# Five single-use weight buffers kept in the ring, 8 KB rows for the last expert's second weights, and another order in the first stages of a one-core block kernel

## The chip, the cores and the metric

The kernel runs on one core of a Trainium2 chip. The metric is the device time of one execution in microseconds. Before the change three runs took 1821.74, 1823.43 and 1823.79 us, so the median is 1823.43 us.

## The reference, cut to what matters

Two transformer blocks on 256 tokens of width 1024, in fp32. The first mixes by a gated 31-tap convolution and neighbourhood attention and ends in a mixture of 16 experts, each on its 32 best tokens. The second (sparse attention, a multi-layer perceptron, latent attention, a second perceptron) is not touched by the change.

```python
sh1, sc1, g1, sh2, sc2, g2 = adaln(c, w_mod[l], b_mod[l])
h = modulate(rms_norm(x, norm_mix_g[l]), sh1, sc1)
hc = modulate(rms_norm(ctx, norm_mix_g[l]), csh1, csc1)
u, q, k, v = jnp.split(h @ w_in[l], splits, axis=-1)
k_c, v_c = jnp.split(hc @ w_in[l][:, splits[1]:], 2, axis=-1)
y_conv = conv_mixer(u, conv_w[l], conv_b[l], conv_ln_g[l], conv_ln_b[l])
y_attn = na_attention(q, k, v, k_c, v_c, rpb[l], idx)
x = x + g1 * (jnp.concatenate([y_conv, y_attn], axis=-1) @ w_out[l])
x = x + g2 * ec_moe(modulate(rms_norm(x, norm_ffn_g[l]), sh2, sc2), ...)
```

An expert is `silu(xs @ w_gate) * (xs @ w_up)` and then `@ w_down`. Its three matrices hold 8 MB each, and every byte of them is read once.

## The kernel before, in words

**Order.** The order of the work on each engine is that in which the program text records it (a manual schedule). Each engine works its instructions off in that order; an instruction that waits holds up everything behind it on its engine.

**Weights.** All weights go through one list `loads` (L105 to L182), nearly all pieces of 1 MB, in the order of use. `pump` (L203) issues the next load on SP's queue as soon as its buffer is free, `take` (L219) hands a landed piece to the code, `free` (L226) gives its buffer back. SP's queue is in order: a load whose buffer is still read holds back all behind it. L187 to L199 give every load a kind of buffer. Ten buffers form the ring (`rp1` with 6, `rp2` with 4). While expert 0 and 1 are loaded there are eleven more on the right side of the memory, which the first stages used till then: five pools of one buffer for the loads `RS` = 9, 13, 14, 10, 12 (counted from expert 0's first load, number 0) and `rp2b` with six for the loads 15 to 20. Each of these eleven serves one load and is closed when expert 1 begins (`rs.close()`, L1010). An expert has 24 loads: `w_gate` and `w_up` in turn, 8 each (numbers 0 to 15), and 8 of `w_down` (16 to 23). So expert 1 begins at number 24.

**Last expert.** The `w_down` of expert 15 is read by column quarters, in eight loads whose rows are pieces of 1 KB (256 floats), with the four loads of `a_kvi` (the next layer's first weights) between them. A piece of a later weight is split into a high and a low part before use: ScalarE rounds it (`wh`), GpSimd or VectorE takes the rest (`wl`).

**First stages.** `w_mod` by the conditioning (`mod_part`, `mod_copy` on ScalarE, transposes on TensorE and a VectorE addition in `mod_fin`) gives the shifts and scales. `h_chunk` (L564) makes the eight chunks of the normed input, with one PSUM bank for two chunks. `half_mm` (L622) multiplies half a weight slot; `Halves` (L345) splits these halves ahead of use, with three buffers. Four rounds `s` make the gated input of the convolution, then two rounds `b` make q, then v and k follow. `drip` (L616) puts convolution taps on VectorE between other work. The sum of squares of the context runs on GpSimd (`SumSq`, L275); TensorE adds it up (`cols`) between the halves of round 2, and spreads the result (`bcast`) behind that round.

**Attention.** `pipeline` (L323) runs 8 units in a software pipeline; per step `S` (scores), `fin`, `norm` (ScalarE and VectorE scale the probabilities), `soft`, `PV`, `T` (TensorE transposes the probabilities), and then hooks (L801): the rest of `w_mod` (`mods`, `mods_b`), the layer norm of the convolution (`ln_b` to `ln_f`) and the quarters of `w_out` (`wo1`). `ln_f` (L774) is a table load, four SiLUs and a copy on ScalarE and a subtraction on VectorE. The first quarter, `wo1(0)`, doesn't read what `ln_f` writes; the second does.

## Time and profile before

| | before |
|---|---|
| median of 3 runs | 1823.43 us (1821.74 to 1823.79) |
| profiled execution, its own time | 1821.56 us |
| its span | 1819.7 us |
| TensorE busy | 1482.8 us, 81% |
| DMA, mean over the span | 300 GB/s |
| chain that ended last | DMA 49%, TensorE 40%, VectorE 6% |
| mean granted clock of TensorE | 0.878 |

The span is the time from the first to the last instruction of the profiled execution; 1.86 us of its own time lie around it. The page has busy shares in 40 slices of 45.5 us. The slices 7 to 25 (about 290 to 1145 us) are the experts, in which the DMA engines never rest; before and behind them TensorE and what it waits for set the pace.

### The profile page before, as it was taken

To read this page: it belongs to the slowest core of one execution; us is meant where nothing else is said; L and a number is where in the kernel's file an instruction comes from. 1 tells how busy PE (TensorE), PEld (TensorE's weight loads), DVE (VectorE), ACT (ScalarE), POOL (GpSimd) and SP (SyncE) were. 2 spreads that over 40 slices of the span, in tenths; PEclk is the share of its full clock that TensorE was granted. 3 is DMA by queue.
4 is the path that set the end of the run, shared out by engine and by line. 5 is a ranking of instruction groups with operands and counts; after the bars stand their busy time and mean duration, and the time that the engine had idled before them with its cause. 6 is when DMAs were issued, how large, how long until landed. Compare 5 with 4: busy or idle time off the path is not lost.

```text
span 1819.7 us, 22674 instructions
## 1 busy us (share of the span) xinstructions
PE 1482.8 (81%) x9569; PEld 905.2 (50%) x9569; DVE 547.1 (30%) x1028; ACT 425.3 (23%) x645; POOL 302.3 (17%) x137
## 2 busy tenths in 40 slices
PE   5898887677667776777677667797999998999998
PEld 2875832122111111121122111485999997889998
DVE  3894320000000000000000000378544366755333
ACT  3435410000000000000000000354454444455442
POOL 1621210000000000000000000243243334223521
PEclk8999888788788968886778788798999997999999
DMA  9639589999999999999999999971445444225550
GB/s 397 241 123 382 206 359 373 419 416 415 415 418 416 416 415 418 417 415 415 419 416 415 415 418 417 370 279 44 161 167 202 162 139 156 71 94 197 179 181 24
DMA packets 109733, 545.88 MB, mean 300 GB/s; under 512 B 8576, under 2 KB 20224, under 8 KB 68480
## 3 DMA queue, kind: packets, MB, share of 16 engines
q1 hardware_dynamic: 106656, 537.72, 74.7%
q10 hardware_dynamic: 2976, 6.72, 1.0%
q8 instruction: 75, 1.23, 0.3%
q14 instruction: 26, 0.21, 0.0%
HBM read 543.36 MB, written 1.05 MB: 299 GB/s over the span
## 4 chain that ended last, share of the span: by engine, by line
DMA 49%; PE 40%; DVE 6%; ACT 2%; issue 2%; POOL 0%; SPq 0%; ACTq 0%; DVEq 0%; POOLq 0%
DMA moe__w<-in_w_up_dram 29%; DMA moe__w<-in_w_down_dram 16%; PE mlp__psB L95 10%; PE mlp__psA L95 10%; DMA moe__w<-in_w_gate_dram 2%; PE moe__psB L95 2%; PE mlaproj__psA L95 2%; PE index__psA L95 2%; PE qkv__psA L95 2%; PE wout__psA L95 1%; PE mlawo__psA L95 1%; PE qkv__psB L95 1%; PE router__psB L95 1%; PE dsawo__psA L95 1%; PE mlaproj__psB L95 1%
## 5 line engine op out<-in xcount | busy, mean ns | idle before, releaser
L95 PE MATMUL moe__psB<-moe__w,moe__xsT 128*32 128x512 f32 x1920 | 346.2, 819 | 172.8 <-DMA moe__w<-in_w_up_dram 88.4
L95 PEld LDWEIGHTS moe__psB<-moe__w,moe__xsT 128*32 128x32 f32 x1920 | 46.7, 123 | 454.5 <-DMA moe__w<-in_w_up_dram 225.4
L95 PE MATMUL moe__psB<-moe__w,moe__hT 128*32 128x512 f32 (+1 forms) x984 | 220.3, 667 | 57.7 <-DMA moe__w<-in_w_down_dram 46.0
L1021 DVE TENSOR_TENSOR moe__hid<-moe__hid,moe__psB 128x512 f32<-128x512 f32 x15 | 10.3, 688 | 575.1 <-PE moe__psB L95 575.1
L303 POOL TENSOR_TENSOR dsaproj__wl<-moe__w,dsaproj__wh 128x1680 fp32r<-128x1680 f32 x4 | 15.2, 3795 | 939.6 <-ACT dsaproj__wh L301 939.6
L95 PEld LDWEIGHTS moe__psB<-moe__w,moe__hT 128*32 128x32 f32 x984 | 52.7, 120 | 214.9 <-DMA moe__w<-in_w_down_dram 121.7
L95 PE MATMUL mlp__psA<-mlp__hh,mlp__wl 128*128 128x256 f32 x512 | 145.0, 283 | 0.0
L95 PE MATMUL mlp__psA<-mlp__hh,mlp__wh 128*128 128x256 f32 x512 | 144.9, 283 | 0.0
L95 PE MATMUL mlp__psA<-mlp__hl,mlp__wh 128*128 128x256 f32 x512 | 144.9, 283 | 0.0
L1020 ACT ACTIVATE moe__hid<-moe__psB 128x512 f32<-128x512 f32 x15 | 9.0, 597 | 535.8 <-PE moe__psB L95 535.8
L95 PE MATMUL mlp__psB<-mlp__xgh,mlp__wh 128*128 128x256 f32 x448 | 125.5, 280 | 0.0
L95 PE MATMUL mlp__psB<-mlp__xgl,mlp__wh 128*128 128x256 f32 x448 | 125.1, 279 | 0.0
L95 PE MATMUL mlp__psB<-mlp__xgh,mlp__wl 128*128 128x256 f32 x448 | 125.0, 279 | 0.0
L301 ACT ACTIVATE mlp__wh<-mlp__w 128x2048 fp32r<-128x2048 f32 (+1 forms) x50 | 94.9, 1899 | 73.2 <-PE mlp__psA L95 55.2
L303 POOL TENSOR_TENSOR mlp__wl<-mlp__w,mlp__wh 128x2048 fp32r<-128x2048 f32 (+1 forms) x17 | 78.0, 4591 | 173.7 <-ACT mlp__wh L301 173.7
L305 DVE TENSOR_TENSOR mlp__wl<-mlp__w,mlp__wh 128x2048 fp32r<-128x2048 f32 (+1 forms) x33 | 75.7, 2292 | 87.6 <-ACT mlp__wh L301 87.6
L95 PEld LDWEIGHTS mlp__psA<-mlp__hh,mlp__wh 128*128 128x128 f32 x512 | 98.2, 192 | 0.0
L95 PEld LDWEIGHTS mlp__psA<-mlp__hh,mlp__wl 128*128 128x128 f32 x512 | 98.1, 192 | 0.0
L95 PEld LDWEIGHTS mlp__psA<-mlp__hl,mlp__wh 128*128 128x128 f32 x512 | 98.1, 192 | 0.0
L1060 DVE COPY moe__ys<-moe__psB 128x512 f32<-128x512 f32 x15 | 10.4, 691 | 251.1 <-PE moe__psB L95 251.1
L95 PEld LDWEIGHTS mlp__psB<-mlp__xgh,mlp__wh 128*128 128x128 f32 x448 | 84.2, 188 | 0.0
L95 PEld LDWEIGHTS mlp__psB<-mlp__xgh,mlp__wl 128*128 128x128 f32 x448 | 84.1, 188 | 0.0
(632 smaller groups left out, 2634.1 us busy)
## 6 DMA issues: line engine op xcount, KB each, us to landing
moe__w<-in_w_down_dram SPq DMA_DIRECT2D x123, 1024.0 KB, 20.0
moe__w<-in_w_gate_dram SPq DMA_DIRECT2D x120, 1024.0 KB, 19.9
moe__w<-in_w_up_dram SPq DMA_DIRECT2D x120, 1024.0 KB, 19.9
mlp__w<-in_mlp_down_dram SPq DMA_DIRECT2D x28, 1024.0 KB, 5.0
mlp__w<-in_mlp_up_dram SPq DMA_DIRECT2D x20, 1024.0 KB, 4.9
qkv__w<-in_w_mod_dram SPq DMA_DIRECT2D x9, 1024.0 KB, 5.1
start__w<-in_w_mod_dram SPq DMA_DIRECT2D x8, 1024.0 KB, 13.6
mod__w<-in_w_mod_dram SPq DMA_DIRECT2D x6, 1024.0 KB, 10.9
```

Of the source, the lines that this page charges most:

```text
L95: nc.tensor.matmul(o, lhsT, rhs, start=start, stop=stop, skip_group_check=True)
L301: nc.scalar.activation(h[:, 0:n], f, AF.Copy)
L303: nc.gpsimd.tensor_tensor(out=l[:, 0:n], in0=f, in1=h[:, 0:n].bitcast(F32), op=ALU.subtract)
L305: nc.vector.tensor_tensor(out=l[:, 0:n], in0=f, in1=h[:, 0:n].bitcast(F32), op=ALU.subtract)
L1020: nc.scalar.activation(hid, gp, AF.Silu)
L1021: nc.vector.tensor_mul(hid, hid, up)
L1060: nc.vector.tensor_copy(ys[1], yp[1])
```

## The change

- **Ring.** The five single-use buffers join the ring after their first load, so the loads 36 and up take turns in 15 buffers instead of 10, until the last expert's `w_down` (`n1`), whose loads use the first ten alone. `rp2b` stays a single-use pool and has a stack of its own, closed when expert 1 begins; the five are closed at the last expert.
- **Last expert.** Its `w_down` comes from a second, repacked input `w_dl`, in which each of the eight pieces has 8 KB contiguous rows. The size is the same.
- **First stages.** The first weight half is rounded ahead of `mod_copy`; the splits 2 to 4 are spread over the chunks; each chunk has a PSUM bank of its own; `cols` and the rest of the context's statistics move behind round 3, `bcast` between the halves of the first `b` round, the context's chunks from 4+4 to 3+5; `drip` does 10, 10, 12 instead of 9, 9, 11; two small VectorE products go to expert 1.
- **Attention.** `mods_b` becomes `mods_cp` (copy) and, some work later, `mods_fin` (transposes). `ln_f` moves from step 5 to step 6, behind `wo1(0)`.

```diff
-ld(1, rows(I["w_down"][e], s % 2 * 1024, slice(q * 256, (q + 1) * 256), 8), 8, 256)
+ld(1, I["w_dl"][s].rearrange("p (k f) -> p k f", k=8), 8, 256)
...
+    slots = [0] * R1 + [1] * R2
     for n, (big, _, _) in enumerate(loads):
-        if n - n0 in RS:
-            ring.append(3 + RS.index(n - n0))
-        elif n0 + RB <= n < n0 + RB + R4:
+        o = n - n0
+        if RB <= o < RB + R4:
             ring.append(2)
-        elif big:
-            ring.append(0 if nb % (R1 + R2) < R1 else 1)
-            nb += 1
+            continue
+        if o in RS:
+            ring.append(3 + RS.index(o))
         else:
-            ring.append(0)
+            if n >= n1:
+                slots = [r for r in slots if r < 2]
+            ring.append(slots.pop(slots.index(0) if not big else 0))
+        slots.append(ring[n])
...
             mod_part(mps, range(6, 8))
+            wst.ahead(1)
             mcol = mod_fin(0, mod_copy(mps))
...
-                if c % 2 == 0:
-                    hts.append(bank("B"))
-                t = half(hts[-1], c % 2)
+                t = half(bank("B"), 0)
...
-                elif s == 2:
-                    cps = bank("B")
-                    ssc.cols(cps)
-                    rc_ = stat_rs(cps)
...
-                elif s == 2:
-                    bcast(rb, rc_, T)
+                elif s == 3:
+                    cps = bank("B")
+                    ssc.cols(cps)
+                    rc_ = stat_rs(cps)
...
-                h_ctx(range(4 * b, 4 * b + 4))
+                if b:
+                    h_ctx(range(3, 8))
                 half_mm(ps, 0)
+                if b == 0:
+                    bcast(rb, rc_, T)
+                    h_ctx(range(0, 3))
                 half_mm(ps, 1)
...
-0: [mods_b(1), mods(range(0, 4))], 1: [mods(range(4, 8)), ln_b], 2: [mods_b(2), ln_c, wsa(1)],
-3: [mods_c, ln_d, wsa(2)], 4: [ln_e, wsa(3)], 5: [ln_f], 6: [wo1(0)], 7: [wo1(1)], 8: [wo1(2)]
+0: [mods_cp, mods(range(0, 4)), mods_fin(1)], 1: [mods(range(4, 8)), ln_b], 2: [mods_cp, ln_c, wsa(1)],
+3: [mods_fin(2), mods_c, ln_d, wsa(2)], 4: [ln_e, wsa(3)], 6: [wo1(0), ln_f], 7: [wo1(1)], 8: [wo1(2)]
```

On SP's queue the loads keep their order. What changes is the place in the program at which each is issued; the number at the end of a tile's name tells it, since names are numbered as the text is recorded. Here are loads 29 to 35 before. Expert 0's `hT`, with which its `w_down` begins, is number 2263, and expert 1's first matmul follows number 2364.

```order
L214 DMA moe__w_2185<-in_w_up_dram 128x2048
L214 DMA moe__w_2204<-in_w_gate_dram 128x2048
L214 DMA moe__w_2298<-in_w_up_dram 128x2048
L214 DMA moe__w_2304<-in_w_gate_dram 128x2048
L214 DMA moe__w_2310<-in_w_up_dram 128x2048
L214 DMA moe__w_2370<-in_w_gate_dram 128x2048
L214 DMA moe__w_2376<-in_w_up_dram 128x2048
```

And with the change, where the numbers of the same two places are 2279 and 2377:

```order
L217 DMA moe__w_2191<-in_w_up_dram 128x2048
L217 DMA moe__w_2197<-in_w_gate_dram 128x2048
L217 DMA moe__w_2208<-in_w_up_dram 128x2048
L217 DMA moe__w_2214<-in_w_gate_dram 128x2048
L217 DMA moe__w_2225<-in_w_up_dram 128x2048
L217 DMA moe__w_2231<-in_w_gate_dram 128x2048
L217 DMA moe__w_2237<-in_w_up_dram 128x2048
```

From load 31 on (the third row) the issue moves from expert 0's `w_down` and expert 1's first pieces to the time of expert 0's `w_gate` and `w_up`.

ScalarE in the first stages before, behind the copy of the first `w_mod` product and up to the first sigmoid (`sg`); `wh` are weight halves, `hh` chunks of the input, and in brackets stands whose semaphore a row waits for:

```order
L572 ACTIVATE rms__hh_137<-uproj__psB_237,mod 128x256 [waits DVE_49] x2
L358 ACTIVATE uproj__wh_242<-start__w_96 128x1024 [waits DMAHW4_49]
L358 ACTIVATE uproj__wh_249<-start__w_96 128x1024
L358 ACTIVATE uproj__wh_255<-start__w_98 128x1024 [waits DMAHW5_49]
L572 ACTIVATE rms__hh_137<-uproj__psB_265,mod 128x256 [waits DVE_49] x2
L572 ACTIVATE rms__hh_137<-uproj__psB_284,mod 128x256 [waits DVE_49] x2
L358 ACTIVATE uproj__wh_297<-start__w_98 128x1024 [waits PE_49,Activation_49]
L572 ACTIVATE rms__hh_137<-uproj__psB_309,mod 128x256 [waits DVE_49] x2
L634 ACT_TABLE_LOAD
L634 ACTIVATE uproj__sg_336<-uproj__psA_248 128x256 [waits PE_49]
```

And with the change, from the second chunk on; the first `wh` now stands ahead of the copy, three rows further up:

```order
L579 ACTIVATE rms__hh_137<-uproj__psB_244,mod 128x256 [waits DVE_49]
L361 ACTIVATE uproj__wh_248<-start__w_96 128x1024
L579 ACTIVATE rms__hh_137<-uproj__psB_262,mod 128x256 [waits DVE_49]
L579 ACTIVATE rms__hh_137<-uproj__psB_272,mod 128x256 [waits DVE_49]
L579 ACTIVATE rms__hh_137<-uproj__psB_282,mod 128x256 [waits DVE_49]
L361 ACTIVATE uproj__wh_286<-start__w_98 128x1024 [waits DMAHW5_49]
L579 ACTIVATE rms__hh_137<-uproj__psB_296,mod 128x256 [waits DVE_49]
L579 ACTIVATE rms__hh_137<-uproj__psB_306,mod 128x256 [waits DVE_49]
L361 ACTIVATE uproj__wh_310<-start__w_98 128x1024 [waits PE_49,Activation_49]
L579 ACTIVATE rms__hh_137<-uproj__psB_322,mod 128x256 [waits DVE_49]
L643 ACT_TABLE_LOAD [waits PE_49]
L643 ACTIVATE uproj__sg_341<-uproj__psA_255 128x256 [waits Activation_49]
```

The other `wh` are spread between the chunks, and the wait for TensorE that stood at the sigmoid now stands at the table load ahead of it.

ScalarE around `ln_f` (L777 and L778) in attention before; `pr` are probabilities, `ts` their transposes, L522 the scaling that the next transposes of TensorE need:

```order
L532 ACTIVATE na__ts_1544<-na__psB_1539 128x512
L532 ACTIVATE na__ts_1551<-na__psB_1546 128x512
L777 ACT_TABLE_LOAD
L777 ACTIVATE rms__y_123<-rms__y_123,vec 128x256 x4
L778 ACTIVATE qkv__mixh_1093<-rms__y_123 128x1024
L522 ACTIVATE na__pr_1521<-na__pr_1521,na__sm_1520 128x512
L511 ACT_TABLE_LOAD
L511 ACTIVATE na__pr_1568,na__sm_1567<-na__psA_1508,na__nmx_1566 128x512
```

And with the change, where `ln_f` is L789 and L790 and the scaling L532:

```order
L521 ACTIVATE na__pr_1568,na__sm_1567<-na__psA_1514,na__nmx_1566 128x512
L521 ACTIVATE na__pr_1574,na__sm_1573<-na__psA_1515,na__nmx_1572 128x512
L542 ACTIVATE na__ts_1591<-na__psB_1586 128x512
L542 ACTIVATE na__ts_1598<-na__psB_1593 128x512
L361 ACTIVATE wout__wh_1628<-mod__w_1171 128x1024
L789 ACT_TABLE_LOAD
L789 ACTIVATE rms__y_123<-rms__y_123,vec 128x256 x4
L790 ACTIVATE qkv__mixh_1099<-rms__y_123 128x1024
L532 ACTIVATE na__pr_1568<-na__pr_1568,na__sm_1567 128x512
```

`ln_f` is passed by one unit's scaling and exponentials and now stands behind the rounding of `w_out`'s fourth half (`wout__wh`), ahead of the last unit's scaling.

## Rows read from the trace of the kernel before

**Rows 1.** The page: DMA rate over 40 slices, and the chain that ended last.

```profile
GB/s 397 241 123 382 206 359 373 419 416 415 415 418 416 416 415 418 417 415 415 419 416 415 415 418 417 370 279 44 161 167 202 162 139 156 71 94 197 179 181 24
...
DMA 49%; PE 40%; DVE 6%; ACT 2%; issue 2%; POOL 0%; SPq 0%; ACTq 0%; DVEq 0%; POOLq 0%
```

**Rows 2.** Us, busy time (count) of PE, PEld, DVE, ACT, POOL, clock, DMA share, GB/s.

```profile
250.00:260.00 10.00, 10.00 (x83) 4.29 (x83) 2.26 (x6) 1.62 (x2) 0.00 (x0) 1.00 1.02 420
260.00:270.00 10.00, 9.22 (x72) 4.98 (x74) 3.01 (x5) 1.52 (x3) 0.00 (x0) 1.00 0.61 252
270.00:280.00 10.00, 8.16 (x47) 5.55 (x43) 2.00 (x3) 1.75 (x3) 0.00 (x0) 1.00 0.81 315
280.00:290.00 10.00, 10.00 (x91) 3.58 (x93) 0.00 (x0) 0.00 (x0) 0.00 (x0) 1.00 0.65 252
400.00:1100.00 700.00, 496.14 (x2444) 114.65 (x2438) 28.00 (x47) 13.74 (x23) 0.00 (x0) 0.81 1.02 416
```

**Rows 3.** Timeline of SP's queue, 196 to 292 us: start, us, what is issued.

```profile
205.82 0.33 SPq L214 DMA_DIRECT2D wout__w<-in_w_gate_dram  x1
...
270.19 0.33 SPq L214 DMA_DIRECT2D moe__w<-in_w_up_dram  x1
...
282.40 0.33 SPq L214 DMA_DIRECT2D moe__w<-in_w_gate_dram  x1
```

**Rows 4.** Timeline of TensorE, 255 to 292 us: start, us, operation [idle before, releaser].

```profile
255.39 2.78 PE L95 MATMUL router__psB<-wout__w,router__xs 128*32 128x512 f32 x24
...
264.72 4.08 PE L95 MATMUL moe__psB<-router__w,moe__hT 128*32 128x512 f32 x34 [0.78 <-DVE moe__hT L1033]
...
281.27 10.51 PE L95 MATMUL moe__psB<-moe__w,moe__xsT 128*32 128x512 f32 x96
```

**Rows 5.** Waits of TensorE, 27 to 130 us: us in total, times, longest.

```profile
PE uproj__psB L95 <- POOL uproj__sqa L286: 3.1, 1, 3.1
PE uproj__psA L95 <- DVE rms__hl L573: 2.4, 2, 1.3
PE qkv__psA L95 <- POOL qkv__wl L360: 1.9, 1, 1.9
PE rms__psB L95 <- DVE uproj__r L266: 1.0, 1, 1.0
```

**Rows 6.** Timeline of GpSimd, 40 to 86 us: first and last of five without idle.

```profile
45.79 2.41 POOL L360 TENSOR_TENSOR uproj__wl<-mod__w,uproj__wh 128x1024 fp32r<-128x1024 f32 x1 [2.55 <-ACT uproj__wh L358]
...
55.98 4.72 POOL L360 TENSOR_TENSOR uproj__wl<-mod__w,uproj__wh 128x1024 fp32r<-128x1024 f32 x2
```

**Rows 7.** Timeline of ScalarE, 26 to 62 us: the table load before the first sigmoid.

```profile
42.21 1.28 ACT L634 ACT_TABLE_LOAD   x1
44.38 0.38 ACT L634 ACTIVATE uproj__sg<-uproj__psA 128x256 f32<-128x256 f32 x1 [0.89 <-PE uproj__psA L95]
```

**Rows 8.** Waits of TensorE, 130 to 206 us.

```profile
PE na__psB L530 <- ACT na__pr L522: 6.3, 2, 6.0
PE mod__psB L445 <- ACT mod__ms L439: 3.2, 2, 1.9
```

**Rows 9.** Timeline of ScalarE, 178 to 200 us: ln_f, then a unit's scaling.

```profile
181.84 1.28 ACT L777 ACT_TABLE_LOAD   x1
...
188.18 0.72 ACT L522 ACTIVATE na__pr<-na__pr,na__sm 128x512 f32<-128x512 f32 x1 [1.89 <-DVE na__sm L518]
...
195.13 1.06 ACT L358 ACTIVATE wout__wh<-mod__w 128x1024 fp32r<-128x1024 f32 x1 [2.49 <-PE wout__psA L95]
```

**Rows 10.** Timeline of TensorE, 178 to 207 us: first quarter of w_out, next transposes.

```profile
190.58 0.56 PE L95 MATMUL wout__psA<-qkv__mixh,convln__wh 128*128 128x256 f32 x1
...
199.47 1.09 PE L530 MATMUL na__psB<-cst,na__pr 128*128 128x128 f32 x8
```

**Rows 11.** The busy-time view again, for the first w_down loads of the last expert.

```profile
1150.00:1160.00 10.00, 7.85 (x48) 3.28 (x40) 1.70 (x3) 1.88 (x2) 0.05 (x1) 0.51 1.06 352
```

**Rows 12.** Timeline of TensorE, 1149 to 1166 us: its last wait for w_down.

```profile
1163.64 1.94 PE L95 MATMUL moe__psB<-moe__w,moe__hT 128*32 128x256 f32 x16 [1.81 <-DMA moe__w<-in_w_down_dram]
```

61 lines of the change are left out of this document (36 added, 25 removed).

## The prediction, made before the changed kernel was run

> **What bounds the kernel now.** I read the page first, then the busy times by stretch, then the timelines at the places where something other than the stream of weights sets the pace. The page's rate is 415 to 419 GB/s from the eighth slice to the twenty-fifth, and DMA has 49% of the chain that ended last [rows 1]. So from about 205 us to 1183 us the time is that of a stream of weights; what starts the stream earlier, takes a hole out of it or shortens it, shortens the kernel. The steady stretch moves 416 GB/s [rows 2], so a load of 1 MB (1.049 MB in decimal units) takes 2.52 us. Nothing is to be had there but by fewer bytes, and the change moves the same bytes.
>
> There is one hole. From 250 to 260 us the stream runs at 420 GB/s, then at 252, 315 and 252 for 10 us each [rows 2]. Ahead of the stream stand the first stages and attention, which TensorE, VectorE, GpSimd and ScalarE pace in turn; the stream for the experts begins for good with the load issued at 205.82 us, which the second quarter of `w_out` releases [rows 3]. Behind it, TensorE sets the pace.
>
> **The hole (ring).** The load issued at 270.19 us is number 31. Its buffer is the one ten turns back, and that holds a piece of expert 0's `w_down`, which TensorE begins at 264.72 us [rows 3, 4]. Load 34, issued at 282.40 us, waits for the first piece of expert 1, which TensorE begins at 281.27 us [rows 3, 4]. With the five buffers in the turn, loads 31 to 35 wait for late pieces of expert 0's `w_gate` and `w_up` instead, which are read at about 255 to 259 us [rows 4]. From load 36 on, the buffer is the one fifteen turns back. The stream then stays fed to about load 38; load 39 needs the first piece of expert 1, free from about 282.4 us as load 34 was. In the stream without a hole load 34 would land four loads after load 30, so about 278 us, and load 38 at 288 us. Load 39 is then issued 5.6 us, the time of two loads, before load 38 lands; if that isn't enough, a us or two of the hole are left.
>
> What it is worth: three stretches of 10 us lack 164, 101 and 164 GB/s against 416 [rows 2], 4.29 MB, and at 416 GB/s that is **10.3 us**. From below: 7 us, if load 39 comes late and something of the start is kept. I take **9.5**. Behind it nothing gives it back: from load 40 to the end the stream is the bound, and a ring of 15 doesn't make a load faster or slower as far as the rows go.
>
> **The first stages.** TensorE's waits in 27 to 130 us that the change touches are 3.1 us for GpSimd's sums of squares, 2.4 us for VectorE's low parts of the chunks, 1.9 us for a GpSimd split [rows 5], together 7.4 us. They don't simply vanish. GpSimd works without idle from 45.79 to 60.70 us (splits of 2.4 us and seven additions) [rows 6]. The change takes none of this work away, it only takes TensorE's wait for the additions out from between two halves. So TensorE next waits for the splits behind these additions, which stand in the same queue. I take half of the 3.1 as lost to that. `bcast` now waits in the first `b` round for the statistics of VectorE, which stand behind round 3 there. Before, behind other work, that wait was 1.0 us [rows 5]; bare of it I count 2 more. The chunks of the context then delay ScalarE's next splits. Of the other things: the first rounded half ahead of `mod_copy` moves work out of TensorE's wait for it; the tap counts only fill VectorE.
>
> The table load for the sigmoid took 1.28 us at 42.21 and ended 0.89 us before TensorE released the sigmoid [rows 7], so it was hidden. With the wait moved ahead of it, it lies open, and 0.9 to 1.3 us are added to the first sigmoid. The Trainium skill (ScalarE: Activation LUTs, What ACT_TABLE_LOAD costs) gives a switch about 2.66 us, of which 1.38 are a drain. By that the estimate for this term would be 1.4 us dearer and the whole forecast as much later. The trace doesn't agree: the row has 1.28 us and a second one at 181.84 is followed by its SiLU without a drain [rows 7, 9], and I go by the rows.
>
> Sum: 7.4 less 1.6, 2 and 1: about **3 us**. From below 0 (all comes back at the splits), from above 5 (the additions' wait and the chunks' wait are kept).
>
> **Attention.** TensorE waits 3.2 us in two pieces for `mod_copy` and 6.3 us, 6.0 of it at once, for a unit's scaling (`pr`) [rows 8]. The first copy is split off and TensorE goes on with the next `w_mod` products: 1.3 us less, of which I count **0.8**, since these products meet loads that come in one after another here. The second, 1.9 us: ScalarE has the same copy, square, rounding and scaling in the same order as before, and the next transposes wait for that scaling. I count nothing, with 1.9 as the upper bound.
>
> The 6.0 us at step 6 go, since `ln_f` no longer stands ahead of the scaling. But it stands ahead of the next one. Before, the quarter of `w_out` begins at 190.58 us, and ScalarE rounds its fourth half at 195.13, 4.5 us after, when TensorE has read a buffer free [rows 9, 10]. The next transposes come at 199.47, 8.9 us after the quarter's begin [rows 10]. Now `ln_f` follows that rounding: 4.5 and 1.06 us, then from the table load at 181.84 to the scaling at 188.18 another 6.3, as before [rows 9], and 0.7 for the scaling: 12.7 us after the quarter's begin. So the transposes wait 3.8 us where they waited none, and 6.0 becomes **2.2**. If the quarter runs faster since TensorE comes to it without the long pause, it is up to 4; if the new pause slows what follows it, 0.7.
>
> Attention: 3.0 us, and with the first stages **6 us** (0 to 10) by which the load of 205.82 us, and the whole stream, begins earlier.
>
> **The last expert.** In 1150 to 1160 us, where loads with 1 KB pieces dominate, the rate is 352 GB/s at a DMA share of 1.06 [rows 11]: 2.98 us a load, 0.46 more than the 2.52 of the rows of 4 and 8 KB. TensorE's last wait for these loads ends at 1163.64 us and was 1.81 us [rows 12]. Up to there four of the eight loads count, so 1.8 us; from there TensorE works without such a wait, and what comes earlier finds it busy. I take **1.9** (with the end of a half us of another wait), from below 0, from above 3.7 for all eight. The third `a_kvi` load now waits for GpSimd's split of the first, with the loads behind it; with two loads still in flight between, I count nothing for that. The skill (DMA: Bandwidth & Descriptors, Why small descriptors are slow) gives a fixed three cycles per packet beside 32 bytes a cycle. That is an estimate of 8% for 1 KB, 0.2 us a load and 0.8 instead of 1.9. The rows show 18%, and the rows decide.
>
> **Sum.** 9.5 + 6 + 1.9 = 17.4 us. The profiled execution took 1821.56 us, 1.87 under the median of 1823.43. So 1804.2 by its own time, **1806.0** as a median.
>
> **The rivals.**
> 1. *The early stages give all back.* GpSimd's splits and the transposes behind `ln_f` take the whole 6 us. For it speak the row without idle on GpSimd and the 3.8 us worked out above; against it that 6.0 us of waiting really go. Then 1823.4 - 9.5 - 1.9 = 1812.
> 2. *The hole moves.* The stream stops at load 39 or later, as expert 1 waits on what TensorE does between the experts. Against it: expert 1's first pieces are free within a us of each other from 282.4. Then some 7 of 9.5 are lost and it is 1813; with the first rival 1819.
> 3. *Slower.* Loads into the five buffers of the right side, which take part in every round now, run slower or hold up the queue, which is in order, so one late buffer stops all. Some 350 loads follow. Break-even is 17.4 / 350 = 0.05 us a load, 2% of 2.52. At 4% it is 1823.4 - 17.4 + 35 = 1841. Against it: in 205 to 260 us the eleven right-side buffers were filled and the rate then was still 420 at the end [rows 2]; for it that no row shows them in the steady stretch.
> 4. *The change doesn't do what it says.* SP's order shows that loads 31 to 35 do move ahead of expert 0's `w_down`, so this is all but excluded for the ring. For the 8 KB rows, the rate may turn out to be limited by the `a_kvi` loads between: 1808.
>
> **How the numbers follow.** The forecast with its bounds, 1799 (all upper bounds together) to 1812, 0.74 (with the fourth rival's 1808 in it). The first rival at 1812 and beyond, 0.13; the second, 0.07; slower, 0.03; no change, since several fall together, 0.03. The range is 1799 to 1814 and leaves out the second rival's worst, the third and the very best. About 0.2% (3.6 us) can be told from no change, so faster means under 1819.8: 0.94; within it 0.03; slower 0.03.
>
> **What would show it.** The stretches 250 to 290 us, moved by about 6, should read near 416 GB/s throughout; SP should issue load 31 without the pause of 15 us. The load of 205.82 should be issued at about 200; TensorE should wait some 4 us for `pr` behind the first quarter of `w_out`. The first sigmoid should follow its table load directly. The loads of the last expert should come at 2.5 us, and the wait of 1.81 us be nearly gone. The forecast is wrong if the stream's rate in the steady stretch falls under 410, if a hole stays near expert 1's begin, or if the load of 205.82 stays within 1 us of its place.

## The result, and the profile after

The changed kernel took 1797.02 us in the median of four runs (1790.50 to 1798.28), the kernel before on the same chip 1823.01: a ratio of 0.985 (interval 0.983 to 0.988). Forecast were 1806.0 and a range of 1799 to 1814. The sign and the order of the parts were right; the gain was too small and the range missed by 2 us. One execution of the changed kernel in a later run took 4179.97 us, more than twice any other, and is left out of all that follows.

The page of the changed kernel, rate over 40 slices:

```profile
GB/s 396 266 136 364 256 415 415 415 419 416 415 416 419 415 415 416 419 415 415 417 418 415 415 418 417 404 256 47 165 178 200 159 142 159 71 95 212 185 169 24
```

This profile is of the fastest of the four runs (1790.50 us). The stream reaches 415 GB/s two slices earlier than in [rows 1]: slices six and seven had 359 and 373. The busy-time view of the place of the hole, 9 us earlier than in [rows 2], with the steady stretch in the last row:

```profile
240.00:250.00 10.00, 10.00 (x80) 4.48 (x73) 1.92 (x6) 1.88 (x2) 0.00 (x0) 1.00 1.02 419
250.00:260.00 10.00, 9.22 (x77) 4.49 (x76) 2.33 (x4) 1.26 (x2) 0.00 (x0) 1.00 1.01 419
260.00:270.00 10.00, 8.16 (x40) 5.90 (x32) 2.15 (x5) 1.75 (x3) 0.00 (x0) 1.00 1.02 419
270.00:280.00 10.00, 10.00 (x97) 3.12 (x100) 0.00 (x0) 0.00 (x0) 0.00 (x0) 1.00 1.01 418
400.00:1070.00 670.00, 477.83 (x2340) 111.86 (x2340) 26.31 (x44) 13.31 (x23) 0.00 (x0) 0.80 1.02 416
```

No hole is left, and the steady rate is the 416 of before. SP's queue in the changed kernel, loads 8, 30, 31 and 39:

```profile
196.87 0.33 SPq L217 DMA_DIRECT2D wout__w<-in_w_gate_dram  x1
...
241.32 0.33 SPq L217 DMA_DIRECT2D moe__w<-in_w_gate_dram  x1
...
242.86 0.33 SPq L217 DMA_DIRECT2D moe__w<-in_w_up_dram  x1
...
271.14 0.33 SPq L217 DMA_DIRECT2D moe__w<-in_w_up_dram  x1
```

Load 8, which opens the stream, is issued 8.95 us earlier than in [rows 3] (6 forecast). Load 31 follows load 30 by 1.5 us, where it paused 15 us before. Load 39 is issued 7.8 us before load 38 lands (278.92).

TensorE's waits in the first stages of the changed kernel, 27 to 125 us:

```profile
PE uproj__psA L95 <- POOL uproj__wl L363: 3.4, 2, 2.4
PE mod__psB L449 <- ACT mod__ms L443: 3.0, 1, 3.0
PE qkv__psB L95 <- POOL qkv__wl L363: 1.6, 1, 1.6
PE uproj__psA L95 <- ACT rms__hh L579: 1.5, 1, 1.5
PE rms__psB L95 <- DVE uproj__r L269: 1.2, 1, 1.2
```

The waits for sums of squares and low parts [rows 5] are gone; waits for splits, for `mod_copy` (`ms`; 0.7 us before) and for the chunks (`hh`) have come. ScalarE in the changed kernel, the first sigmoid, and then `ln_f` with the scaling behind it:

```profile
41.18 1.28 ACT L643 ACT_TABLE_LOAD   x1 [1.56 <-PE uproj__psA L95]
42.48 0.39 ACT L643 ACTIVATE uproj__sg<-uproj__psA 128x256 f32<-128x256 f32 x1
...
179.74 1.06 ACT L361 ACTIVATE wout__wh<-mod__w 128x1024 fp32r<-128x1024 f32 x1 [1.35 <-PE wout__psA L95]
180.82 1.28 ACT L789 ACT_TABLE_LOAD   x1
...
187.17 0.72 ACT L532 ACTIVATE na__pr<-na__pr,na__sm 128x512 f32<-128x512 f32 x1 [1.89 <-DVE na__sm L528]
```

The table load now waits and the sigmoid follows it at once, as worked out from [rows 7]. `ln_f` stands behind the rounding, and the scaling behind `ln_f` comes 10.5 us after the quarter's begin at 176.65. TensorE's waits in attention of the changed kernel, then the one behind the first quarter of `w_out` in its timeline:

```profile
PE na__psB L540 <- ACT na__pr L532: 5.1, 2, 3.8
```

```profile
157.41 1.09 PE L540 MATMUL na__psB<-cst,na__pr 128*128 128x128 f32 x8 [1.33 <-ACT na__pr L532]
...
187.94 1.97 PE L540 MATMUL na__psB<-cst,na__pr 128*128 128x128 f32 x8 [3.79 <-ACT na__pr L532]
```

The forecast for the last row was 3.8 us. The waits for `mod_copy` [rows 8] are both gone. The last expert in the changed kernel, rate while its `w_down` lands, and TensorE's last wait for it:

```profile
1130.00:1140.00 10.00, 7.01 (x49) 2.36 (x45) 1.70 (x3) 1.09 (x3) 0.00 (x0) 0.54 1.02 417
```

```profile
1143.24 1.07 PE L95 MATMUL moe__psB<-moe__w,moe__hT 128*32 128x256 f32 x16 [1.17 <-DMA moe__w<-in_w_dl_dram]
```

417 GB/s instead of 352 [rows 11]; the eight loads land 2.50 us apart instead of 2.98.

**Where the time went.** Landing times of transfers are marks on the way. The table gives, for six of them, the time in the profiled execution of before, and for the other profiles the difference to it in us. `k` is the load that the k projection's buffer releases; 8 opens the stream; 39 lies behind the hole; `w_up` is expert 15's last; then the first weight of the index stage (the second block), and `last` the first piece of the output, as it is written. The other names are further profiles of the two kernels and the variants of the experiments, told below.

```
                   k      8     39    w_up    index     last   its time
before        120.33 210.66 301.02 1149.55  1218.42  1813.30    1821.56
c_before1       -0.7   +2.8   +2.7    +2.5     +2.8     -1.7    1819.93
c_before2       -0.6   -0.9   -3.0    -3.2     -3.2    -12.3    1809.26
after           -4.9   -8.9  -19.6   -18.4    -22.1    -30.9    1790.50
after_again     -4.3   -7.7  -18.2   -17.1    -18.9    -23.5    1797.95
after_third     -4.2   -9.4  -18.6   -17.5    -20.7    -26.3    1795.20
e_ring          +0.1   -0.4  -10.5    -9.3     -9.5    -14.6    1806.89
g_ring2         -0.3   +3.0   -2.0    -2.1     -2.0     -7.9    1813.90
e_rows          -0.3   +2.8   +4.2    +4.1     +0.7     +1.0    1822.52
e_first         -3.7   -0.5   -2.3    -2.4     -2.5     -8.6    1812.85
e_attn          -0.8   -5.0   -4.8    -4.9     -4.6     -4.8    1816.78
h_ctx           +2.4   +2.3   +2.2    +2.2     +2.1     +2.1    1823.57
h_head          -4.6   -4.6   -6.3    -6.5     -6.7    -13.9    1807.68
f_lnf           -4.4  -11.4  -21.4   -20.2    -23.4    -23.4    1798.01
c_lnf           -4.7  -11.3  -21.1   -20.1    -23.5    -28.4    1793.03
i_best          -4.4  -12.7  -23.7   -22.5    -25.6    -26.0    1795.47
```

The parts are read between the columns. Behind the index stage the change touches nothing, and still 9 us come in there in the first pair of profiles. That was the open question of the experiments.

### The profile page after: what moved, and what is told of

Same layout as the page of the kernel before. It is cut to its first block, busy times and chain, and to the rows that moved or that the text cites. A ratio compares the mean times of both kernels' runs of the same rounds, so it can differ in the third digit from the quotient of the medians.

```text
span 1788.7 us, 22696 instructions
## 1 busy us (share of the span) xinstructions
PE 1463.3 (82%) x9569; PEld 893.5 (50%) x9569; DVE 544.1 (30%) x1028; ACT 424.1 (24%) x645; POOL 300.1 (17%) x137
## 4 chain that ended last, share of the span: by engine, by line
DMA 50%; PE 36%; DVE 10%; ACT 2%; issue 1%; POOL 0%; ACTq 0%; SPq 0%; DVEq 0%; POOLq 0%
DMA moe__w<-in_w_up_dram 31%; DMA moe__w<-in_w_down_dram 15%; PE mlp__psB L95 11%; PE mlp__psA L95 10%; DVE conv__psA L617 3%; PE moe__psB L95 3%; PE mlaproj__psA L95 2%; PE dsawo__psA L95 1%; PE wout__psA L95 1%; PE mlawo__psA L95 1%; PE router__psB L95 1%; DMA start__w<-in_w_uqk_dram 1%; DMA mod__w<-in_w_out_dram 1%; PE mlaproj__psB L95 1%; ACT mlaatt__ss L1800 1%
## 5 line engine op out<-in xcount | busy, mean ns | idle before, releaser
L95 PE MATMUL moe__psB<-moe__w,moe__xsT 128*32 128x512 f32 x1920 | 342.1, 812 | 168.4 <-DMA moe__w<-in_w_up_dram 87.4
L306 POOL TENSOR_TENSOR dsaproj__wl<-moe__w,dsaproj__wh 128x1680 fp32r<-128x1680 f32 (+1 forms) x4 | 15.9, 3980 | 925.6 <-DMA moe__w<-in_w_dl_dram 916.4
L1075 ACT ACTIVATE moe__ys<-moe__psB 128x512 f32<-128x512 f32 x15 | 9.0, 597 | 317.9 <-PE moe__psB L95 317.9
```

Of the source, the lines that this page charges most:

```text
L95: nc.tensor.matmul(o, lhsT, rhs, start=start, stop=stop, skip_group_check=True)
L306: nc.gpsimd.tensor_tensor(out=l[:, 0:n], in0=f, in1=h[:, 0:n].bitcast(F32), op=ALU.subtract)
L1075: nc.scalar.activation(ys[0], yp[0], AF.Copy)
```

## The experiments

### Each part alone

Ring alone (the loop over `loads`, `rs4`, the later `rs.close()`):

```diff
+        if o in RS:
+            ring.append(3 + RS.index(o))
+        else:
...
+        slots.append(ring[n])
```

> The kernel before with the ring change alone (five buffers stay in the turn; the pool of six has its own stack). From the landings of the two traces: the ring is worth 10.7 us, so about 1812.3 against 1823.0, and the load after number 31 comes without a pause. By the forecast's term, 9.5. Rival (the parts only work together: without the earlier start the stream stops at load 39 all the same): under 7. Rival (the ring lets TensorE's clock or the later stages run differently): over 12.

1807.7 us in the median against 1820.7 for the kernel before (ratio 0.994, 0.992 to 0.995). Load 39 lands 10.5 us earlier, with the stream opened at the same time (-0.4). The place of the hole in this run:

```profile
260.00:270.00 10.00, 9.22 (x71) 4.84 (x73) 2.97 (x5) 1.27 (x2) 0.00 (x0) 1.00 1.01 421
270.00:280.00 10.00, 8.15 (x45) 5.73 (x38) 2.00 (x3) 1.75 (x3) 0.00 (x0) 1.00 1.01 419
280.00:290.00 10.00, 10.00 (x93) 3.33 (x95) 0.00 (x0) 0.00 (x0) 0.00 (x0) 1.00 1.00 415
```

The hole is filled to the end, not to load 38 with a rest as the forecast allowed for. The stream keeps most of it: 9.3 us are left 850 us on. By the medians the part would be worth 13.0 us, which falls in the last rival's range; the profile has 9.5 of its 14.6 us at the index stage, and 5.0 come in behind it, where this edit changes nothing.

8 KB rows alone:

```diff
-ld(1, rows(I["w_down"][e], s % 2 * 1024, slice(q * 256, (q + 1) * 256), 8), 8, 256)
+ld(1, I["w_dl"][s].rearrange("p (k f) -> p k f", k=8), 8, 256)
```

> The kernel before with the repacked w_down of the last expert alone. From the traces: the loads come at 2.5 instead of 2.97 us, and up to the first wait of the index stage 3.7 us are gained, so about 1819.3. By the forecast's term, 1.9: 1821.1. Rival (the later gains of the changed kernel's profile, 1.7 us around the first attention's output and 6.3 us in the latent attention's projections, come from this part, through what stands behind it): 1811 to 1818.

Time 1817.72 (0.999, 0.998 to 1.001): not told from no change, although the median lies 3.0 us under that of before, in the rival's range. The profile is of the slowest of the twelve executions (1822.52), whose stream opened 2.8 us late. Its landings tell the part: from `w_up` to the index stage it gains 3.4 us. The rival needs a gain behind the index stage, and there is none (+0.3). The stretch with the loads in this run, against 352 in [rows 11]:

```profile
1153.00:1163.00 10.00, 5.68 (x52) 2.17 (x48) 2.73 (x6) 3.17 (x5) 0.51 (x1) 0.89 1.02 418
```

First stages alone (all edits ahead of attention, context part included):

```diff
+            wst.ahead(1)
             mcol = mod_fin(0, mod_copy(mps))
...
-                t = half(hts[-1], c % 2)
+                t = half(bank("B"), 0)
...
+                elif s == 3:
+                    cps = bank("B")
```

> The kernel before with the new order of the first stages alone. From the traces: the k projection ends 4.8 us earlier, of which 2.4 are waits of TensorE and the rest a clock that is granted earlier and lost less. Attention and the stream should keep it: about 1818.2. By the forecast's term, 3: 1820. Rival (attention gives it back at the w_mod loads, which come one after another): 1822 to 1823.

1815.81 us (0.998, 0.997 to 0.999). The k projection's load lands 3.7 us earlier, but at load 8 only 0.5 us are left. Attention's program is that of the kernel before. Its busy-time view in the kernel before, and then here, 4 us earlier:

```profile
160.00:170.00 10.00, 9.09 (x69) 7.19 (x70) 4.93 (x14) 6.84 (x12) 4.46 (x2) 1.00 1.02 419
170.00:180.00 10.00, 8.93 (x55) 6.50 (x55) 8.93 (x27) 5.59 (x11) 2.49 (x2) 0.83 0.86 354
```

```profile
156.00:166.00 10.00, 8.75 (x57) 7.19 (x58) 3.63 (x12) 7.28 (x13) 3.54 (x2) 0.79 1.02 418
166.00:176.00 10.00, 9.74 (x44) 6.68 (x44) 6.55 (x24) 4.33 (x9) 1.60 (x2) 0.70 0.89 362
```

The granted clock was 0.79 and 0.70 where it had been 1.00 and 0.83. So the loss of 3.2 us lies where TensorE ran in part at 1.2 GHz. Nine profiles have attention's old program. In five of them the mean granted clock between `k` and load 8 is 0.94, and the stretch takes 89.9 to 90.4 us; in the other four (c_before1, g_ring2, e_rows and this one) it is 0.89 to 0.91, and the stretch takes 93.4 to 93.8. The head alone (below) is one of the five and kept all 4.6 us, so the loss isn't bound to the earlier start.

Attention alone:

```diff
-2: [mods_b(2), ln_c, wsa(1)],
-3: [mods_c, ln_d, wsa(2)], 4: [ln_e, wsa(3)], 5: [ln_f], 6: [wo1(0)],
+2: [mods_cp, ln_c, wsa(1)],
+3: [mods_fin(2), mods_c, ln_d, wsa(2)], 4: [ln_e, wsa(3)], 6: [wo1(0), ln_f],
```

> The kernel before with mods_cp, mods_fin and the later ln_f alone. From the traces: 1.4 us up to the transposes of unit 3, and 2.8 from there to the release of the load that opens the stream, together 4.1: about 1818.9. By the forecast's term, 3.0: 1820. TensorE waits 3.8 us for pr behind the first quarter of w_out, as in the changed kernel. Rival (without the first stages' gain the copy is no longer covered by w_mod loads that land in time): about 2.

1810.83 us (0.995, 0.992 to 0.997). Load 8 lands 5.0 us earlier, 4.3 of them from attention itself, and 4.6 us are left at the index stage. Forecast were 3.0. The median is no price here: the seven executions lie at 1803.66 to 1805.38, 1810.83 and 1816.55 to 1816.78, and the profile is of the slowest.

The four parts add up by stages: 9.1 us for the ring from load 8 on, 3.4 for the rows, 3.7 for the first stages up to `k` and 4.3 for attention are 20.5, and the three profiles of the changed kernel have 20.6 at the index stage in the mean. By the medians the four would be 30.7, against 23.4 for the whole change in the run of the same kernel below.

### A ring with fewer of the five

Only the buffers of loads 9 and 10 stay in the turn:

```diff
-        slots.append(ring[n])
+        if o not in RS[1:3] + RS[4:]:
+            slots.append(ring[n])
```

> The kernel before with the ring change, but with two of the five buffers kept in the turn instead of five (loads 13, 14 and 12 stay the only ones of theirs). By the mechanism of the hole: loads 31 and 32 go ahead, 33 to 35 wait for expert 0's w_down, 36 for expert 1; the stream is dry for 2 to 5 us instead of 10, and load 39 lands 6 to 8 us earlier than before. Rival (each buffer is worth the time of one load that comes early, 5 of them 10.5): 4.2 us. Rival (any wait left on the queue keeps the hole): under 2.

1811.49 us (0.996, 0.994 to 0.997). From load 30 to load 39 it gains 5.6 us, where the whole ring gains 10.6. Two rows of this run:

```profile
270.00:280.00 10.00, 8.69 (x62) 4.48 (x52) 1.27 (x2) 1.27 (x3) 0.00 (x0) 1.00 0.96 361
280.00:290.00 10.00, 9.46 (x72) 4.80 (x76) 0.74 (x2) 0.48 (x1) 0.00 (x0) 1.00 0.65 257
```

A part of the hole stays, and it stands later. SP's queue in this run, loads 32, 33 and 36:

```profile
257.89 0.33 SPq L218 DMA_DIRECT2D moe__w<-in_w_gate_dram  x1
273.10 0.33 SPq L218 DMA_DIRECT2D moe__w<-in_w_up_dram  x1
...
285.31 0.33 SPq L218 DMA_DIRECT2D moe__w<-in_w_gate_dram  x1
```

Loads 31 and 32 go ahead, 33 pauses for 15 us and 36 for another 10, at the places that the expectation named; so the reasoning by turns of the ring holds. Its price missed: 5.6 us lies between the theory's 6 to 8 and the rival's 4.2. Each buffer gave 2 to 3 us.

### The pause behind ln_f

The changed kernel with `ln_f` ahead of the first quarter of `w_out`, run twice:

```diff
-4: [ln_e, wsa(3)], 6: [wo1(0), ln_f], 7: [wo1(1)], 8: [wo1(2)]
+4: [ln_e, wsa(3)], 6: [ln_f, wo1(0)], 7: [wo1(1)], 8: [wo1(2)]
```

> The changed kernel with ln_f recorded ahead of the first quarter of w_out instead of behind it, one line. ScalarE then does ln_f while TensorE reads the quarter's first half, and the rounding of the fourth half comes behind it. Theory (ln_f only has to lie under the 6 to 7.4 us of that quarter, and it stood behind a rounding that waits for TensorE): the 3.8 us for pr are gone, and the load that opens the stream is issued 3 to 5 us earlier; the time is about 3.5 us less than after_again. Rival (VectorE's part of ln_f or the late rounding of the fourth half becomes the next wait, or the clock gives it back): less than 1 us.

The two waits that took the place of the 3.79 us:

```profile
185.85 0.66 PE L540 MATMUL na__psB<-cst,na__pr 128*128 128x128 f32 x4 [1.38 <-ACT na__pr L532]
...
187.08 0.89 PE L540 MATMUL na__psB<-cst,na__pr 128*128 128x128 f32 x4 [0.57 <-DVE na__pr L530]
```

Load 8 lands 3.7 us earlier than in the run of the changed kernel beside it, and 2.7 us earlier than the mean of that kernel's three profiles. So 1.8 us of waiting less (3.79 against 1.38 and 0.57) gave 2.7 to 3.7 us, with a granted clock of 0.96 over the stretch from `k` to load 8, where the changed kernel's three profiles have 0.94, 0.94 and 0.96. At the index stage the gain is still there (-23.4 and -23.5 against -20.6 in the mean). The medians show less: 1795.56 us against 1796.21, under the 1 us of the rival. What became of it is the next question.

### Is the rest the change's or the execution's?

The same kernels again: the changed one twice, the one before twice, the variant above once more. No edit.

> The changed kernel once more, unaltered, to see how it scatters and on the same chip as the kernels beside it. Theory: by the landings of the profiles the change is worth 22 to 24 us up to the index stage (early stages 8 to 9, ring 10.5, 8 KB rows 3.5 to 4), and what its first profile showed beyond that is TensorE's clock in the latent attention, which some executions of either kernel have. Then its runs lie 22 to 26 us under those of before, in two groups about 6 us apart, and a profile that lands in the upper group shows about 24.5 us at the end. Rival (the later gain belongs to the change): all runs near 1790 and 30 us under before.

> The changed kernel once more, beside the one above on the same chip, so that their medians can be compared: 1791 to 1798 us, in the two groups seen so far (near 1791 and near 1796 to 1798). If the groups come from the granted clock in latent attention, as the theory says, a profile near 1791 shows 0.8 or more in the projections there after TensorE's pause for the columns, and one near 1797 shows 0.5 to 0.6 in part of them. The rival, that they come from the DMA stream, expects the load that opens the index stage to differ by the 6 us already.

> The kernel before, unedited, for another profile of it. Theory: the granted clock of TensorE in the projections of latent attention, 1527 to 1557 us (0.58, 0.50, 0.90 in the profile of before, 0.66 to 0.83, 0.83 and 1.00 in three profiles of the changed kernel) differs from execution to execution of one kernel; then a profile of this kernel whose time is in its lower group (1810 to 1816 us) shows 0.66 or more, 0.83 and 1.00 there, and one of 1818 to 1824 us the lower row. Rival: the row is the kernel's own (it was low in six profiles and high in seven, by kernel); then every profile of this kernel shows 0.58, 0.50, 0.90, and the two groups of its times come from elsewhere.

> As for the run before it, a further profile of the same kernel: by the theory the higher clocks with a time of 1810 to 1816 us and the lower with 1818 to 1824; by the rival 0.58, 0.50, 0.90 whatever the time.

> The changed kernel with the norm's last step ahead of the first quarter of w_out, once more. Its first profile had the low row (0.58, 0.50, 0.90) at 1798.0 us, although its stream began 2.5 to 3.7 us earlier than in the three profiles of the changed kernel. By the theory that the row is drawn anew in each execution it may be high now, and the time is then 1791 to 1793 us; by the rival it is low again, and the time 1795 to 1798 us.

After_again had 1796.21 us (1791.07 to 1797.95), 23.4 under before, as its theory had it; after_third had 1795.92 (1795.05 to 1800.93, five executions). The two of the kernel before took 1819.93 and 1809.26 us, the variant 1793.03.

In latent attention, far behind the change, TensorE stands 3.6 us for VectorE's columns in the traces of either kernel and then works on. The busy-time view from there, in the profile of before:

```profile
1527.00:1537.00 10.00, 8.94 (x32) 7.81 (x33) 7.72 (x17) 2.89 (x5) 0.70 (x1) 0.58 0.30 105
1537.00:1547.00 10.00, 10.00 (x47) 9.97 (x48) 1.76 (x1) 3.40 (x3) 0.00 (x0) 0.50 0.31 105
1547.00:1557.00 10.00, 10.00 (x80) 10.00 (x80) 6.20 (x29) 5.53 (x6) 0.00 (x0) 0.90 0.01 2
```

In the changed kernel's first profile:

```profile
1502.40:1512.40 10.00, 8.95 (x52) 8.10 (x52) 7.72 (x17) 4.96 (x7) 0.69 (x1) 0.83 0.32 105
1512.40:1522.40 10.00, 10.00 (x73) 10.00 (x73) 4.65 (x15) 4.50 (x5) 0.00 (x0) 0.83 0.30 107
```

And in c_before2, which is the kernel before:

```profile
1521.00:1531.00 10.00, 8.97 (x52) 8.13 (x52) 7.70 (x17) 4.97 (x7) 0.67 (x1) 0.83 0.32 105
1531.00:1541.00 10.00, 10.00 (x74) 10.00 (x74) 4.67 (x15) 4.49 (x5) 0.00 (x0) 0.83 0.33 107
```

47 matmuls in 10 us at a granted 0.50, 73 or 74 at 0.83. One kernel has either row, so the clock there differs from execution to execution: 0.58, 0.50, 0.90 or 0.66, 0.83, 1.00 or 0.83, 0.83, 1.00, and between the first and the last lie 6.3 us. The variant had the first row with 1798.01 us and the second with 1793.03. The rival (every execution of a kernel has the kernel's own row) falls. That the row is drawn by chance alone isn't shown: the six executions of the ring alone lie within 1.2 us of each other, and those of the kernel before within 15. Two sentences of the theory missed: c_before1 had 1819.93 us with the middle row, since its stream had opened 2.8 us late, and after_again had 1797.95 with the middle one too, and so had after_third with 1795.20. This one place doesn't make the two groups of times by itself; the index stage is another, with granted clocks of 0.66, 1.00, 0.66 or about 0.72, 0.97, 0.87, and 2 to 3 us between them.

With the same later row on both sides, after (1790.50) and c_before2 (1809.26) differ by 18.8 us, and by 18.9 at the index stage already. It is one pair: c_before2's own hole was 2.2 us shorter than that of the first profile. The nine pairs of three profiles each differ by 15.7 to 24.9 us at the index stage, 20.4 in the mean.

### Taking the first stages apart

The context part alone (its statistics behind round 3, `bcast` in the first `b` round, chunks 3+5):

```diff
-                elif s == 2:
+                elif s == 3:
                     cps = bank("B")
...
-                h_ctx(range(4 * b, 4 * b + 4))
+                if b:
+                    h_ctx(range(3, 8))
                 half_mm(ps, 0)
+                if b == 0:
+                    bcast(rb, rc_, T)
+                    h_ctx(range(0, 3))
```

> The kernel before with one part of the first stages' change alone: the context's statistics behind round 3, bcast within the first b round, its chunks 3 and 5. Theory (GpSimd's splits pace these rounds, so the wait for the additions comes back as waits for splits and for bcast): the k projection ends 0 to 1.5 us earlier, and TensorE waits for splits in rounds 2 and 3. Rival (this is the part that carries the 3.7 to 4.9 us): 3 us or more. The end of the k projection is read by the landing of the last load before attention's, 120.33 us before.

It loses: the k projection's load comes 2.4 us later (one execution), and both the theory (0 to 1.5 us earlier) and the rival (3 or more) missed. The seven other profiles with the first stages of before lie within 0.9 us of each other there, so the loss is clear of that scatter. Its waits of TensorE, 27 to 130 us:

```profile
PE uproj__psA L95 <- POOL uproj__wl L360: 2.3, 1, 2.3
...
PE qkv__psB L95 <- POOL qkv__wl L360: 1.9, 1, 1.9
PE qkv__psB L95 <- ACT qkv__wh L358: 1.4, 1, 1.4
...
PE qkv__psA L95 <- POOL qkv__wl L360: 1.0, 1, 1.0
```

The 3.1 us for the sums of squares [rows 5] are gone, and these have come for it or grown: `uproj__wl` is new, `qkv__wl` is 2.9 us in two waits where it was 1.9, `qkv__wh` 1.4 where it was 0.5. From 30 us to `k` TensorE's idle time is 0.7 us longer than before, and the mean granted clock is 0.908 instead of 0.924, about 1.7 us over this stretch. The head alone, that is all other edits of the first stages:

```diff
+            wst.ahead(1)
             mcol = mod_fin(0, mod_copy(mps))
...
+                if k in (2, 4):
+                    wst.ahead(3 + (k - 2) // 2)
...
-                    drip(9 if s < 2 else 11)
+                    drip(10 if s < 2 else 12)
```

> The kernel before with the first-stage part of the change, its context rows left where they stood: the weight splits spread over the opening, a bank for each chunk, the longer drip, the modulation products moved, but the context's statistics, broadcast and first three chunks ahead of the first query product as before. Alone the whole first-stage part ended the last k projection's load 3.7 us earlier, and the context part by itself 2.4 us later. Theory A, the parts add: the landing that ends the k projection (120.33 us in the kernel before) comes 6.1 us earlier, at about 114.2. Theory B, the context move pays only together with the spread splits, because the drip it makes room for is longer: less than 3.7 us earlier, 116.6 or later. In the waits of TensorE between 27 and 125 us A expects a sum near 10 us or below and no wait for the context's ACT copies over 2 us; B a new wait for ACT or DVE rows of the context.

4.6 us earlier (one execution), between the two theories (6.1, and less than 3.7). Its two largest waits:

```profile
PE uproj__psB L95 <- POOL uproj__sqa L286: 4.4, 1, 4.4
PE mod__psB L446 <- ACT mod__ms L440: 3.0, 1, 3.0
```

The wait for the sums of squares is back and longer, and the end of the k projection is where the whole part has it (-3.7 to -4.9). So with the head the context part is worth nothing that can be told, and without it it costs 2.4. The whole gain of the first stages is the head's; its own edits were not run apart.

Both findings in one kernel: the changed one with `ln_f` ahead of the quarter, and the context part as before.

```diff
-4: [ln_e, wsa(3)], 6: [wo1(0), ln_f], 7: [wo1(1)], 8: [wo1(2)]
+4: [ln_e, wsa(3)], 6: [ln_f, wo1(0)], 7: [wo1(1)], 8: [wo1(2)]
...
-                if b:
-                    h_ctx(range(3, 8))
+                h_ctx(range(4 * b, 4 * b + 4))
                 half_mm(ps, 0)
-                if b == 0:
-                    bcast(rb, rc_, T)
-                    h_ctx(range(0, 3))
```

> The changed kernel with two edits: the norm's last step is issued ahead of the first quarter of w_out (the pause of 3.79 us became 1.38 us in the run of that edit alone), and the context part stands as in the kernel before. Theory A, the parts of the first stages add: the k projection's end is 2 to 2.5 us earlier than in the changed kernel (115.4 us, so about 113), and the stream's opener some 5 to 6 us earlier than the changed kernel's 201.7, at about 196; medians of the runs 3 to 6 us below the changed kernel's. Theory B, the context move is needed with the spread splits: the k projection's end is at 115.4 us or later, and the opener only the 3.7 us or less of the norm's edit earlier, medians within 1.5 us of the run with the norm's edit alone.

1795.69 us (1791.42 to 1796.78), the variant with `ln_f` alone 1795.56. The k projection's end is not earlier, the opener 3.8 us earlier than in the changed kernel: the second theory. By landings this is the best of all up to the index stage (-25.6), 3.5 us ahead of the changed kernel's best; its profile then had the low row in latent attention, and the medians are within 2 us of the changed kernel's. Whether it beats it isn't shown.

## Why the prediction was right or wrong

The main mechanisms held, and the time fell outside the range by the sizes of some terms and by a base that was taken too high. Attention was put at 3.0 us because of the two waits for `mod_copy` the second was counted as nothing and the first as 0.8; the two gave 1.9, and the stage measured 4.1 by waits and 5.3 in the mean. The last expert was put at 1.9 because what stands behind TensorE's last wait was counted as nothing; it measured 3.0. And the median of before was 3.6 us lower than the three runs that the forecast started from. Means over three profiles of either kernel, taken from the table between its columns:

```
stage                          forecast   measured
first stages (to k)                 3.0        4.0
attention (k to load 8)             3.0        5.3
hole (load 8 to 39)                 9.5        9.3
stream (39 to w_up)                 0         -1.2
last expert (w_up to index)         1.9        3.0
later stages (index to last)        0          1.8
sum                                17.4       22.2
```

The 1.8 us of the later stages lie where the change touches nothing and go with the mean granted clock there: 0.966, 0.971 and 0.977 in the profiles of before, 0.977, 0.971 and 0.971 in those of the changed kernel.

**The ring: right.** The gain is the shortfall of the stretches in [rows 2] and the mechanism the one by turns of the ring. The rest of a hole at load 39 that the forecast allowed for didn't come. The second rival (the hole moves) falls with the row of 419 GB/s.

**The stream: right, to 1 us.** Some 350 loads lost 1.2 us together, 0.003 us each. The third rival needed 0.05.

**First stages: the balance of the waits was nearly right, by other waits than named, and the clock was left out.** Forecast was 7.4 us less 4.6 for what comes back. TensorE's busy time from 30 to 120 us is a direct reading; before and then after, sums over the 10 us stretches of the busy-time view:

```profile
sum 90.00, PE 78.17 PEld 70.85 DVE 72.68 ACT 38.21 POOL 50.36; mean PE 8.69 PEld 7.87 DVE 8.08 ACT 4.25 POOL 5.60
```

```profile
sum 90.00, PE 81.37 PEld 72.71 DVE 78.21 ACT 37.00 POOL 50.30; mean PE 9.04 PEld 8.08 DVE 8.69 ACT 4.11 POOL 5.59
```

TensorE has 3.2 us less idle time; the other 1.7 of this pair's 4.9 is the granted clock, 0.89 and 0.94 from 70 to 90 us before and 1.00 after. In the mean of three profiles it is 2.6 us of idle time. The step "TensorE next waits for the splits", with half of the 3.1 us for the sums of squares kept, was too kind: the waits for splits went from 1.9 to 5.0 us, which is all of it, and alone that edit loses 2.4 us. What I had not counted is a wait that the spread of the weight splits takes away. It stands first in the waits of TensorE of before, 27 to 130 us:

```profile
PE uproj__psA L95 <- ACT uproj__wh L358: 3.5, 1, 3.5
```

I had looked at the first half's rounding only as work moved into the wait for `mod_copy`, which grows in return from 0.7 to 3.0 us. The 2 us counted for `bcast` didn't come (1.0 and 1.2 us), and 1.5 us for the chunks (`hh`) did. So that the sum of 3 came near 4.0 is in good part luck: the waits that it named give 0.7 us net. The table load lay open as forecast. Of the Trainium skill (ScalarE: Activation LUTs, What ACT_TABLE_LOAD costs) the row shows no drain of 1.38 us: 1.28 us and the sigmoid 0.02 us behind it, as in the profile of before the SiLU at 183.13 is 0.01 us behind the load of 181.84.

**Attention: one term exact, one too small.** "6.0 becomes 2.2" came out: a pause of 3.79 us is left. That it is exact is a cancellation. The quarter ran at full clock in 6.0 us; TensorE was ready for the transposes 7.5 us after its begin instead of 8.9, and the scaling ended after 11.2 instead of 12.7. Both ends moved by 1.4 us, so a faster quarter didn't shorten the pause, as "up to 4" supposed. The failing step is "I count nothing" for the second copy, and 0.8 of 1.3 for the first. Both waits for `mod_copy`, 3.2 us, went; what came back was 1.33 us for a scaling at 157.41. Net 1.9 and 2.2 by waits is 4.1. What stands above that in the mean is the clock: of the profiles of before one, with 0.91 instead of 0.94, lost 3.4 us between `k` and load 8 against the first. Against the five profiles of the old program at 0.94 (90.2 us in the mean) the new program, in the changed kernel's three profiles and in attention alone (0.94 to 0.96), takes 86.1, and 4.1 are left.

**Last expert: right up to the fourth load, and what stands behind it was put at nothing.** From the landing of `w_up` to that of the fourth `w_down` load, with which TensorE's last wait ends, it is 14.0 us in each of the nine profiles with 1 KB rows and 12.1 in each of the seven with 8 KB rows, whatever the granted clock was: 2.0 us, and 1.9 were forecast. The wait of [rows 12] itself went from 1.81 to 1.17 us, not to nearly nothing, and after_third has 1.34 of it and 1.98 at the load before: where TensorE runs faster it comes earlier and waits longer, so the length of one wait wasn't the measure. The failing step is "what comes earlier finds it busy": from the fourth load to the index stage another 1.0 us is gained in the mean, and 1.7 in the first pair. By what isn't shown. In the first pair the granted clock of the 12 us behind that load differs:

```profile
1163.60:1175.60 12.00, 11.96 (x108) 9.38 (x109) 6.03 (x12) 5.31 (x10) 3.90 (x2) 0.87 1.06 352
```

```profile
1143.20:1155.20 12.00, 11.03 (x109) 9.05 (x110) 6.86 (x12) 6.92 (x13) 5.82 (x2) 1.00 0.91 362
```

That would be about 1.5 us. But the rows alone gained 1.4 us there with these two stretches of 6 us, in the mean 0.86 and so the clock of before:

```profile
1165.60:1171.60 6.00, 5.85 (x42) 4.50 (x42) 1.99 (x4) 1.99 (x2) 1.30 (x2) 0.72 1.02 416
1171.60:1177.60 6.00, 6.00 (x67) 4.87 (x66) 4.71 (x8) 3.73 (x8) 3.15 (x1) 1.00 1.02 419
```

The eight loads gain 0.48 us each, where 0.46 were read from [rows 11]. The `a_kvi` loads between them gain another 1.5 us, but 1.3 of that is the second of them, which takes 3.4 us before and 2.1 in the changed kernel; it takes 3.5 with the rows alone and 2.2 with the ring alone, so it goes with the ring and not with the rows. An estimate by the Trainium skill's fixed three cycles a packet (DMA: Bandwidth & Descriptors, Why small descriptors are slow) would have been 0.8 for the term; the trace doesn't agree, 2.98 against 2.50 us a load.

**The median.** The forecast stood on three runs of before between 1821.74 and 1823.79 us. Over 59 executions the kernel before has a median of 1819.87 (1809.26 to 1824.16), and the changed one over 15 has 1796.57 (1790.50 to 1800.93): 23.3 us apart, near the 22.2 of the table. So of the miss of 9.0 us 4.8 are in the stages (1.8 of them behind the change), 3.6 in the three runs I counted from, and the rest in the few runs of the result. The upper bounds of the terms were added up to 1799 and so held the stages, but nothing was left for the scatter. Rival 1 (the early stages give all back) falls with load 8 at 196.87 us, rival 4 with the rates.

Open: why the clock comes out differently in two executions of one program, and whether a kernel's timing makes one row more frequent. Three profiles of either kernel don't show it. The narrow times of the ring alone speak for it, and so do the counts in attention: four of the nine profiles of its old program had 0.89 to 0.91 there, and none of the seven with the new order, the variants included, was under 0.94. Nothing was run to test it.

## What to carry to other kernels

In front of a stream that is the bound TensorE's waits count, and so does the clock, which cost 3.4 us in attention in some executions; read TensorE's busy sum over the whole stretch instead of adding up named waits, because a wait that is removed in an in-order queue comes back under another name. Take an edit apart before you keep it: of the first stages' two groups of edits one carried all of the gain and the other was a loss by itself. Compare executions by landing times at stage borders, not by totals, where later stages that nobody touched differed by up to 9 us from one execution to the next.

## What the runs showed of the hardware that was not expected

The granted clock of TensorE behind one and the same pause of 3.6 us was 0.58 and 0.50 in the two stretches of 10 us behind it in some executions (0.50 is 1.2 GHz), and 0.66 and 0.83 or 0.83 and 0.83 in others of the same program, worth 3.2 or 6.3 us of 1.8 ms. The stream from HBM did not care which buffers it filled: 416 GB/s over ten buffers and over fifteen. And loads of 1 MB with 1 KB rows landed 2.98 us apart, with 8 KB rows 2.50.
